# Attention in an fp32 encoder: the product of probabilities and v as plain fp32 on two 64-column halves of the array

## Chip, core and metric

The kernel runs on one core of one Trainium2 chip. The metric is device time in microseconds (us) of one execution, the median of several; lower is better. The output has to agree with a float32 reference.

The engines are named as the profile names them: PE is TensorE's matmul side, PEld its weight loads, DVE is VectorE, ACT ScalarE, POOL GpSimd, SP SyncE (which only issues DMAs here). In a matmul row, "128*128 128x256" means 128 rows by 128 columns of the array in use and a moving operand of 128 partitions by 256 elements.

## The reference

Two layers of an encoder over 512 tokens of width 1024, each a half-step FFN, a mixer of neighbourhood attention and a Fourier branch, and a second half-step FFN; a final RMSNorm. The change is in the attention: 8 heads of 64 channels on a grid of 8 rows by 64 columns of tokens. Queries come in 4 blocks of 16 grid columns, each with a band of 32 columns of keys. A block is 8 x 16 = 128 queries, a band 8 x 32 = 256 keys.

```python
s = jnp.einsum('brjqhd,brjuvhd->brjhquv', qg, k_win).astype(jnp.float32) * scale + bias[None]
s = jnp.where(col_ok[None, None, :, None, :, None, :], s, -jnp.inf)
sh = s.shape
p = jax.nn.softmax(s.reshape(sh[:-2] + (kh * KEY_BAND_COLS,)), axis=-1).reshape(sh)
o = jnp.einsum('brjhquv,brjuvhd->brjqhd', p.astype(v.dtype), v_win)
```

The last line is the product that the change touches: probabilities times the values of the band.

## The kernel before

**Numbers in two parts.** Nearly every product in the kernel is made in three passes. An operand x is split into a high part hi, which ScalarE writes in the type fp32r (a copy that rounds), and a low part lo = x - hi, which VectorE writes. `mm3` (L314 to L317) then issues hi*hi, hi*lo and lo*hi into one PSUM accumulation. `hilo` makes one buffer of 512 KB with room for both parts; all such buffers, and the weights of the mixer stage, share one pool of 23 buffers (tag "k", `slot`, L111). PSUM has 8 banks of 512 fp32 columns (`bank`, L118).

**Weights.** `ws` streams weights from HBM: SP and POOL issue the loads, ScalarE writes the high parts (whi), VectorE the low parts (wlo), a few granules ahead of TensorE.

**Attention in chunks.** The work comes in eight chunks i = 0 to 7: hp = i // 2 is a pair of heads (their 2 x 64 channels fill the 128 partitions) and pr = i % 2 a pair of query blocks. For each chunk the steps are:

- `att_scores` (L1264): scores of both heads. The two heads lie in the two halves of the partitions, so each matmul uses 64 rows of the array, and the calls alternate between the heads (e = 0, 1).
- `Probs`: bias, maximum, exponential, sum and scaling, on VectorE and ScalarE.
- `transposed` (L1311): eight fp32 transposes on TensorE (L1317) bring keys onto the partitions. For each of the two blocks jj, one PSUM bank then holds 512 columns: key half c = 0, 1, and in each half the 128 queries of head 0 and the 128 of head 1.
- `high_of` (L1094): ScalarE copies such a bank to SBUF as the high part (L1097), VectorE subtracts to make the low part (L1100). Both are named p.
- `att_pv` (L1324): for each block and key half, `mm3` with v as the stationary operand, 128 columns (both heads), and the 256 columns (both heads' queries) as the moving one: 12 matmuls of 256 columns a chunk. The result has a row of blocks of which only those with a head's own v and its own queries are used.
- `att_split` (L1336): picks these blocks out of PSUM, one ScalarE copy (L1342) and one VectorE subtraction (L1345) for each head, and writes the two parts of o.

**v.** A projection leaves four 128-token blocks of values. `v_high` (L1107) scales them into a high part on ScalarE (L1109), `v_low` (L1111) makes the low part on VectorE (L1112). Bands that straddle two blocks need a shifted copy: three buffers vs, each filled by two DMAs from SP (L1554, L1555).

**Order.** The whole attention stands in a manual schedule: the order of work on TensorE, VectorE and ScalarE is the order of the program text. Between the attention's steps stand the Fourier branch (`four_*`, `rotated`, `rows_of`), the projections (`proj_T`) and the preparation of weights. `att_pv` is called for two chunks in a row each time, so there are four such pairs in a layer: (0, 1) between the last key projection and transposes, the others among `rows_of`. Next comes the gate stage (`gate_block`), with products in the same three passes. `flip` (L475) holds a plain fp32 matmul, one call in each layer, with 2 moving columns.

Of the kernel before, what the change touches and what calls it, by code (L numbers as in the profile page):

```python
# [9 lines left out]
F32 = mybir.dt.float32  # L10
F32R = mybir.dt.float32r
# [23 lines left out]
BAND = (0, 1, 3, 4)  # L35
# [55 lines left out]
def encoder_kernel(  # L91
    ctx: ExitStack, tc: tile.TileContext, xin, xtr, wst, gains, gfin, gbias, bias_in, dft, chan, ident_in, rot, out
):
    nc = tc.nc
    V, S, G, PE = nc.vector, nc.scalar, nc.gpsimd, nc.tensor
# [218 lines left out]
    def mm3(ps, lh, ll, rh, rl, start, stop, again=False):  # L314
        PE.matmul(ps, lh, rh, start=start, stop=False, skip_group_check=again)  # L315
        PE.matmul(ps, lh, rl, start=False, stop=False, skip_group_check=again)  # L316
        PE.matmul(ps, ll, rh, start=False, stop=stop, skip_group_check=again)  # L317
# [717 lines left out]
    def stage_mixer(l, norm, nxt):  # L1035
# [58 lines left out]
        def high_of(t, s):  # L1094

            hi, lo = hilo(s)
            S.activation(hi, t, AF.Copy)  # L1097

            def low_of():
                V.tensor_tensor(lo, t, hi.bitcast(F32), ALU.subtract)  # L1100
                return hi, lo

            return low_of

        vt = [None] * TB

        def v_high(b, src):  # L1107
            vt[b] = slot(F32R, "v", (2, T))
            S.activation(vt[b][:, 0, :], src, AF.Copy, scale=norm.r[:, b : b + 1])  # L1109

        def v_low(b, src):  # L1111
            V.scalar_tensor_tensor(  # L1112
                vt[b][:, 1, :], src, norm.r[:, b : b + 1], vt[b][:, 0, :].bitcast(F32), ALU.mult, ALU.subtract
            )

        def proj_UV():

# [137 lines left out]
        o, q, k, bms = [], {}, {}, {}  # L1255
# [55 lines left out]
        def transposed(s_):  # L1311
# [9 lines left out]
                res.append(pt)  # L1321
            return res

        def att_pv(i, p_):  # L1324
            hp, pr = divmod(i, 2)
            po = bank()
            hs = slice(hp * P, (hp + 1) * P)
            for jj in range(2):
                ph, pl = p_[jj]
                for c in range(2):  # L1330
                    vh, vl = vch[BAND[2 * pr + jj] + 2 * c]
                    cs = slice(c * 256, (c + 1) * 256)
                    mm3(po[:, jj * 256 : jj * 256 + 256], vh[:, hs], vl[:, hs], ph[:, cs], pl[:, cs], c == 0, c == 1)
            return po

        def att_split(i, po):  # L1336
            hp, pr = divmod(i, 2)
            pv = po.rearrange("p (a e q) -> p a e q", a=2, e=2)
            oh, ol = [z[:, pr * 256 : pr * 256 + 256].rearrange("p (a q) -> p a q", a=2) for z in o[hp]]
            for e in range(2):  # L1340
                r = slice(64 * e, 64 * e + 64)
                S.activation(oh[r], pv[r, :, e, :], AF.Copy)  # L1342
            for e in range(2):
                r = slice(64 * e, 64 * e + 64)
                V.tensor_tensor(ol[r], pv[r, :, e, :], oh[r].bitcast(F32), ALU.subtract)  # L1345


        def rows_of(src, tb, w, kts=range(4), ps=None):
# [141 lines left out]
        with tc.manual_schedule(engines={mybir.EngineType.DVE, mybir.EngineType.Activation}):  # L1490
            with tc.manual_schedule(engines={mybir.EngineType.PE}):
                u, k1, pa, sb, acts4 = proj_UV()
# [24 lines left out]
                product(pa, acts4, K4, False, again=True, ahead=0)  # L1517
                q[2] = q2()
                for c in range(2):
                    v_high(c, pa[c])  # L1520
                f0, f1 = four_ch(b_[0]), four_ch(b_[1])
                g0, g1 = four_q(f0[1]), four_q(f1[1])
                for c in range(2):
                    v_low(c, pa[c])
                bias_for(1)
                p1.exps(1)
                fp = [four_pos(2), four_pos(3)]
# [3 lines left out]
                p1.inverse(1)  # L1531
                k2 = proj_T(None, 0)
                for c in range(2):
                    v_high(2 + c, sb[:, c, :])
                y0 = four_high(y0)
                y1 = four_high(y1)
                bt = [rotated(fp[0])]
# [8 lines left out]
                b_ = [bh[0](), bh[1]()]  # L1546
                k2 = k2()
                ws.prep(ws.pos + 2)
                for c in range(2):
                    v_low(2 + c, sb[:, c, :])  # L1550
                vs = []
                for s in range(3):
                    t = slot(F32R, "vs", (2, T))
                    nc.sync.dma_start(out=t[0:64].bitcast(F32), in_=vt[s][64:128].bitcast(F32))  # L1554
                    nc.sync.dma_start(out=t[64:128].bitcast(F32), in_=vt[s + 1][0:64].bitcast(F32))  # L1555
                    vs.append(t)
                fq = []

# [10 lines left out]
                w1 = four_high(w1)  # L1569
                yf += [y0(), y1()]  # L1570
                ts = transposed(p0.s) + transposed(p1.s)
                ph = [high_of(t, "p") for t in ts]
                q3 = q3()
                ph = [h() for h in ph]
                pt_ = {0: ph[0:2], 1: ph[2:4]}
                p2, p3 = [Probs(i, att_scores(i)) for i in (2, 3)]
                k3 = proj_T(None, 0)
                p2.maxes(0)
# [19 lines left out]
                p3.scaled(1)  # L1598
                k3 = k3(False)
                bias_for(2)  # L1600
                vch = {i: (t[:, 0, :], t[:, 1, :]) for i, t in ((0, vt[0]), (1, vs[0]), (2, vt[1]), (3, vs[1]), (4, vt[2]), (5, vs[2]), (6, vt[3]))}
# [6 lines left out]
                ph = [high_of(t, "p") for t in ts[0:2]]  # L1608
                pt_[2] = [h() for h in ph]
# [4 lines left out]
                pt_[3] = [h() for h in ph]  # L1614
# [28 lines left out]
                ph = [high_of(t, "p") for t in ts[0:2]]  # L1643
                pt_[4] = [h() for h in ph]
                att_split(2, po[0])
                att_split(3, po[1])
                second_f = [ws.next(0)]
# [1 line left out]
                p6.maxes(0)  # L1649
                ws.prep(ws.pos + 1)  # L1650
                p6.maxes(1)
                ph = [high_of(t, "p") for t in ts[2:4]]
                pt_[5] = [h() for h in ph]
                p6.exps(0)
                p7.maxes(0)
                p6.inverse(0)
# [24 lines left out]
                ph = [high_of(t, "p") for t in ts[0:2]]  # L1681
                pt_[6] = [h() for h in ph]
                att_split(4, po[0])
                att_split(5, po[1])
                ph = [high_of(t, "p") for t in ts[2:4]]
# [5 lines left out]
                po = [att_pv(i, pt_.pop(i)) for i in (6, 7)]  # L1691
# [61 lines left out]
        pa = pair("wA")  # L1753
# [230 lines left out]
```

## Time and profile before

| | |
|---|---|
| median of 3 timed runs | 1870.2 us (1869.01 to 1872.32) |
| profiled execution, device time | 1872.91 us |
| its span, first to last instruction | 1871.1 us |
| ScalarE busy in the span | 1307.7 us (70%) |
| granted TensorE clock, mean | 0.999 |
| HBM read over the span | 365.85 MB, 197 GB/s |

How to read it. The page of a profile gives busy time for each engine; a share of the span is a mean over stages that have different limits. Matmuls are pipelined: the next starts before the last has ended, so the cost of one is read from start to start, not from its own duration. Rows of the order of time read: start, duration, engine, line, operation, output and inputs by the program's names, shape, count; a row with "x24" stands for 24 like instructions in a row. In brackets stands the idle time ahead of a row and what ended it. The rows on which the argument rests stand in the prediction.

### The profile page before, as it was taken

To read this page: it belongs to the slowest core of one execution; us is meant where nothing else is said; L and a number is where in the kernel's file an instruction comes from. 1 tells how busy PE (TensorE), PEld (TensorE's weight loads), DVE (VectorE), ACT (ScalarE), POOL (GpSimd) and SP (SyncE) were. 2 spreads that over 40 slices of the span, in tenths; PEclk is the share of its full clock that TensorE was granted. 3 is DMA by queue.
4 is the path that set the end of the run, shared out by engine and by line. 5 is a ranking of instruction groups with operands and counts; after the bars stand their busy time and mean duration, and the time that the engine had idled before them with its cause. 6 is when DMAs were issued, how large, how long until landed. Compare 5 with 4: busy or idle time off the path is not lost.

```text
span 1871.1 us, 24628 instructions
## 1 busy us (share of the span) xinstructions
PE 1854.5 (99%) x8830; PEld 1543.7 (82%) x8830; DVE 1638.3 (88%) x2006; ACT 1307.7 (70%) x1788; POOL 171.4 (9%) x210
## 2 busy tenths in 40 slices
PE   9999999999999999999999999999999999999998
PEld 7888878888888888888888888878887888888886
DVE  7877899788989987889998888997889899888899
ACT  6777875668666867777666778666685567677865
POOL 0001011100111001001010100101001101010010
PEclk9999999999999999999999999999999999999999
DMA  9898798932886888879888887988248867888794
GB/s 302 223 236 210 196 255 271 230 103 90 248 219 161 179 225 225 223 195 259 259 196 220 225 219 200 269 266 202 85 139 229 213 166 176 221 227 222 196 283 151
DMA packets 190139, 393.70 MB, mean 210 GB/s; under 512 B 95488, under 2 KB 95616, under 8 KB 190016
## 3 DMA queue, kind: packets, MB, share of 16 engines
q1 hardware_dynamic: 161344, 293.77, 48.8%
q0 software_dynamic: 28528, 98.33, 29.6%
q8 instruction: 69, 1.13, 0.2%
q14 instruction: 54, 0.44, 0.1%
q10 hardware_dynamic: 144, 0.02, 0.0%
HBM read 365.85 MB, written 2.11 MB: 197 GB/s over the span
## 4 chain that ended last, share of the span: by engine, by line
PE 85%; DVE 5%; DMA 5%; issue 4%; ACT 1%; POOL 0%; SPq 0%; DVEq 0%; ACTq 0%; POOLq 0%
PE A L491 10%; PE A L492 10%; PE A L494 10%; PE B L492 5%; PE B L491 5%; PE B L494 5%; PE o L494 5%; PE o L492 5%; PE o L491 5%; DMA raw<-in_wst_dram 4%; PE ps L315 3%; PE ps L316 3%; PE ps L317 3%; PE C L491 2%; PE C L492 2%
## 5 line engine op out<-in xcount | busy, mean ns | idle before, releaser
L194 DVE TENSOR_TENSOR wlo<-raw,whi 128x1024 fp32r<-128x1024 f32 (+1 forms) x534 | 630.8, 1190 | 165.6 <-ACT whi L191 164.2
L191 ACT ACTIVATE whi<-raw 128x1024 fp32r<-128x1024 f32 (+1 forms) x534 | 547.2, 1033 | 270.5 <-DVE raw L164 59.8
L150 POOL DMA_DIRECT2D raw<-in_wst_dram x166 | 144.3, 889 | 1337.4 <-DMA raw<-in_wst_dram 895.5
L164 DVE TENSOR_TENSOR raw<-raw,raw 128x1024 f32<-128x1024 f32 (+1 forms) x150 | 178.5, 1191 | 2.0
L492 PE MATMUL A<-whi,xl 128*128 128x512 f32 x400 | 155.7, 389 | 0.0
L491 PE MATMUL A<-whi,xh 128*128 128x512 f32 x400 | 155.7, 389 | 0.0
L698 ACT ACTIVATE at<-zt 128x1024 uint16<-128x1024 uint16 (+2 forms) x96 | 111.0, 1168 | 20.6 <-DMA zt<-zs 20.6
L186 ACT ACTIVATE whi<-raw 128x1024 fp32r<-128x1024 f32 (+1 forms) x83 | 85.9, 1035 | 50.2 <-PE A L492 13.6
L494 PE MATMUL A<-wlo,xh 128*128 128x512 f32 x400 | 115.0, 389 | 0.0
L187 DVE SCALAR_TENSOR_TENSOR wlo<-raw,whi 128x1024 fp32r<-128x1024 f32 (+1 forms) x83 | 98.2, 1192 | 12.9 <-ACT whi L186 12.8
L494 PEld LDWEIGHTS A<-wlo,xh 128*128 128x128 f32 x400 | 75.1, 188 | 15.6
L491 PEld LDWEIGHTS A<-whi,xh 128*128 128x128 f32 x400 | 75.1, 188 | 15.4
L492 PEld LDWEIGHTS A<-whi,xl 128*128 128x128 f32 x400 | 75.1, 188 | 15.4
L491 PE MATMUL C<-whi,xh 128*128 128x512 f32 x208 | 81.3, 391 | 0.5 <-ACT whi L191 0.5
L492 PE MATMUL C<-whi,xl 128*128 128x512 f32 x208 | 81.0, 389 | 0.0
L492 PE MATMUL B<-whi,xl 128*128 128x512 f32 x208 | 81.0, 389 | 0.0
L491 PE MATMUL B<-whi,xh 128*128 128x512 f32 x208 | 80.9, 389 | 0.0
L681 ACT ACTIVATE zs<-th 128x1024 uint16<-128x1024 uint16 x80 | 79.5, 1042 | 0.9 <-DVE th L729 0.9
L722 ACT ACTIVATE th<-sn,rh 128x512 f32<-128x512 f32 x80 | 55.1, 715 | 35.4 <-DVE sn L566 34.6
L561 ACT ACTIVATE sn<-A 128x512 f32<-128x512 f32 x104 | 59.1, 585 | 23.6 <-PE A L494 23.6
L494 PE MATMUL C<-wlo,xh 128*128 128x512 f32 x208 | 59.8, 389 | 0.0
L494 PE MATMUL B<-wlo,xh 128*128 128x512 f32 x208 | 59.8, 389 | 0.0
(449 smaller groups left out, 4772.0 us busy)
## 6 DMA issues: line engine op xcount, KB each, us to landing
raw<-in_wst_dram SPq DMA_DIRECT2D x470, 512.0 KB, 5.7
raw<-in_wst_dram POOLq DMA_DIRECT2D x174, 512.0 KB, 8.0
raw<-in_wst_dram SPq DMA_DIRECT2D x30, 256.0 KB, 3.5
bm<-in_bias_dram SPq DMA_DIRECT2D x16, 384.0 KB, 3.8
vs<-v SPq DMA_DIRECT2D x12, 256.0 KB, 3.8
x<-in_xin_dram SPq DMA_DIRECT2D x4, 512.0 KB, 10.2
raw<-in_wst_dram POOLq DMA_DIRECT2D x8, 256.0 KB, 8.4
dft<-in_dft_dram POOLq DMA_DIRECT2D x8, 256.0 KB, 4.3
```

The costliest lines, as they stand in the source:

```text
L150: G.dma_start(out=self.t, in_=wst[GRAN_AT[self.plus]][:, 0 : self.n], accum_op=ALU.add)
L164: V.tensor_tensor(self.raw.t, self.raw.t, self.add.t, ALU.add)
L186: S.activation(hi, t, AF.Copy, scale=-1.0)
L187: self.last = V.scalar_tensor_tensor(lo, t, -1.0, hi.bitcast(F32), ALU.mult, ALU.subtract)
L191: S.activation(hi[:, cs], t[:, cs], AF.Copy)
L194: self.last = V.tensor_tensor(lo[:, cs], t[:, cs], hi[:, cs].bitcast(F32), ALU.subtract)
L491: PE.matmul(ps, lh, rh, start=start, stop=False, skip_group_check=again)
L492: PE.matmul(ps, ll, rh, start=False, stop=False, skip_group_check=again)
L494: PE.matmul(ps, lh, rl, start=False, stop=stop, skip_group_check=again)
L561: S.activation(t[:, b, :], ps[b], AF.Copy)
L681: S.activation(s[:, h], words[:, h], AF.Copy)
L698: S.activation(to[:, w, i : i + n, :], t[:, w, q : q + n, :], AF.Copy)
```

## The change

`att_pv` takes v and the probabilities as plain fp32. For each block and key half it issues one matmul for each head: 64 columns of v as the stationary operand, the head's own 128 queries as the moving one, and the output on partitions 0 to 63 or 64 to 127, the halves of the array's columns. A chunk has 8 such calls in place of 12 matmuls of three passes. The output of a chunk is 256 columns in which every block is used, so `att_split` is one copy and one subtraction over all partitions. v and p have no low parts any more: `value` and `kept` make plain fp32 copies on ScalarE. Buffers for v and vs hold half as many bytes, and p has one buffer for a chunk in place of two.

```diff
-        def v_high(b, src):
-            vt[b] = slot(F32R, "v", (2, T))
-            S.activation(vt[b][:, 0, :], src, AF.Copy, scale=norm.r[:, b : b + 1])
-
-        def v_low(b, src):
-            V.scalar_tensor_tensor(
-                vt[b][:, 1, :], src, norm.r[:, b : b + 1], vt[b][:, 0, :].bitcast(F32), ALU.mult, ALU.subtract
-            )
+        def value(b, src):
+            vt[b] = slot(F32, "v", (T,))
+            S.activation(vt[b], src, AF.Copy, scale=norm.r[:, b : b + 1])
...
+        def kept(ts):
+            p_ = slot(F32, "p", (2, T))
+            for jj in range(2):
+                S.activation(p_[:, jj, :], ts[jj], AF.Copy)
+            return p_
+
         def att_pv(i, p_):
             hp, pr = divmod(i, 2)
             po = bank()
-            hs = slice(hp * P, (hp + 1) * P)
             for jj in range(2):
-                ph, pl = p_[jj]
+                js = slice(jj * P, (jj + 1) * P)
                 for c in range(2):
-                    vh, vl = vch[BAND[2 * pr + jj] + 2 * c]
-                    cs = slice(c * 256, (c + 1) * 256)
-                    mm3(po[:, jj * 256 : jj * 256 + 256], vh[:, hs], vl[:, hs], ph[:, cs], pl[:, cs], c == 0, c == 1)
+                    v = vch[BAND[2 * pr + jj] + 2 * c]
+                    for e in range(2):
+                        d = slice(hp * P + 64 * e, hp * P + 64 * e + 64)
+                        cs = slice(c * 256 + e * P, c * 256 + (e + 1) * P)
+                        PE.matmul(po[64 * e : 64 * e + 64, js], v[:, d], p_[:, jj, cs], start=c == 0, stop=c == 1)
             return po
 
         def att_split(i, po):
             hp, pr = divmod(i, 2)
-            pv = po.rearrange("p (a e q) -> p a e q", a=2, e=2)
-            oh, ol = [z[:, pr * 256 : pr * 256 + 256].rearrange("p (a q) -> p a q", a=2) for z in o[hp]]
-            for e in range(2):
-                r = slice(64 * e, 64 * e + 64)
-                S.activation(oh[r], pv[r, :, e, :], AF.Copy)
-            for e in range(2):
-                r = slice(64 * e, 64 * e + 64)
-                V.tensor_tensor(ol[r], pv[r, :, e, :], oh[r].bitcast(F32), ALU.subtract)
+            oh, ol = [z[:, pr * 256 : pr * 256 + 256] for z in o[hp]]
+            S.activation(oh, po[:, 0:256], AF.Copy)
+            V.tensor_tensor(ol, po[:, 0:256], oh.bitcast(F32), ALU.subtract)
...
                 for c in range(2):
-                    v_high(2 + c, sb[:, c, :])
+                    value(2 + c, sb[:, c, :])
...
-                for c in range(2):
-                    v_low(2 + c, sb[:, c, :])
                 vs = []
                 for s in range(3):
-                    t = slot(F32R, "vs", (2, T))
-                    nc.sync.dma_start(out=t[0:64].bitcast(F32), in_=vt[s][64:128].bitcast(F32))
-                    nc.sync.dma_start(out=t[64:128].bitcast(F32), in_=vt[s + 1][0:64].bitcast(F32))
+                    t = slot(F32, "vs", (T,))
+                    nc.sync.dma_start(out=t[0:64], in_=vt[s][64:128])
+                    nc.sync.dma_start(out=t[64:128], in_=vt[s + 1][0:64])
                     vs.append(t)
...
                 ts = transposed(p0.s) + transposed(p1.s)
-                ph = [high_of(t, "p") for t in ts]
+                pt_ = {0: kept(ts[0:2]), 1: kept(ts[2:4])}
                 q3 = q3()
-                ph = [h() for h in ph]
-                pt_ = {0: ph[0:2], 1: ph[2:4]}
...
-                ph = [high_of(t, "p") for t in ts[2:4]]
-                pt_[7] = [h() for h in ph]
+                pt_[7] = kept(ts[2:4])
```

The calls for the other chunks change in the same way, at the places where they stood.

More of the change, by code (lines that the diff above doesn't have):

```diff
@@ L1519, in stage_mixer @@
                 for c in range(2):
-                    v_high(c, pa[c])
+                    value(c, pa[c])
                 f0, f1 = four_ch(b_[0]), four_ch(b_[1])
                 g0, g1 = four_q(f0[1]), four_q(f1[1])
-                for c in range(2):
-                    v_low(c, pa[c])
                 bias_for(1)
@@ L1548, in stage_mixer @@
                 ws.prep(ws.pos + 2)
-                for c in range(2):
-                    v_low(2 + c, sb[:, c, :])
                 vs = []
                 for s in range(3):
-                    t = slot(F32R, "vs", (2, T))
-                    nc.sync.dma_start(out=t[0:64].bitcast(F32), in_=vt[s][64:128].bitcast(F32))
-                    nc.sync.dma_start(out=t[64:128].bitcast(F32), in_=vt[s + 1][0:64].bitcast(F32))
+                    t = slot(F32, "vs", (T,))
+                    nc.sync.dma_start(out=t[0:64], in_=vt[s][64:128])
+                    nc.sync.dma_start(out=t[64:128], in_=vt[s + 1][0:64])
                     vs.append(t)
@@ L1600, in stage_mixer @@
                 bias_for(2)
-                vch = {i: (t[:, 0, :], t[:, 1, :]) for i, t in ((0, vt[0]), (1, vs[0]), (2, vt[1]), (3, vs[1]), (4, vt[2]), (5, vs[2]), (6, vt[3]))}
+                vch = dict(enumerate((vt[0], vs[0], vt[1], vs[1], vt[2], vs[2], vt[3])))
                 o.append(hilo("o"))
@@ L1607, in stage_mixer @@
                 ts += transposed(p3.s)
-                ph = [high_of(t, "p") for t in ts[0:2]]
-                pt_[2] = [h() for h in ph]
+                pt_[2] = kept(ts[0:2])
                 att_split(0, po[0])
@@ L1612, in stage_mixer @@
                 k3 = k3()
-                ph = [high_of(t, "p") for t in ts[2:4]]
-                pt_[3] = [h() for h in ph]
+                pt_[3] = kept(ts[2:4])
                 k[3] = k3()
@@ L1642, in stage_mixer @@
                 ts = transposed(p4.s) + transposed(p5.s)
-                ph = [high_of(t, "p") for t in ts[0:2]]
-                pt_[4] = [h() for h in ph]
+                pt_[4] = kept(ts[0:2])
                 att_split(2, po[0])
@@ L1651, in stage_mixer @@
                 p6.maxes(1)
-                ph = [high_of(t, "p") for t in ts[2:4]]
-                pt_[5] = [h() for h in ph]
+                pt_[5] = kept(ts[2:4])
                 p6.exps(0)
@@ L1680, in stage_mixer @@
                 swap_pools(0)
-                ph = [high_of(t, "p") for t in ts[0:2]]
-                pt_[6] = [h() for h in ph]
+                pt_[6] = kept(ts[0:2])
                 att_split(4, po[0])
                 att_split(5, po[1])
-                ph = [high_of(t, "p") for t in ts[2:4]]
-                pt_[7] = [h() for h in ph]
+                pt_[7] = kept(ts[2:4])
                 ws.prep(ws.pos + 1)
```

## The prediction

> **What bounds the kernel now.** I read the page first, then busy times by stretch, then the order of time on TensorE around the product.
>
> ```profile
> span 1871.1 us, 24628 instructions
> ...
> PE 1854.5 (99%) x8830; PEld 1543.7 (82%) x8830; DVE 1638.3 (88%) x2006; ACT 1307.7 (70%) x1788; POOL 171.4 (9%) x210
> ...
> PE 85%; DVE 5%; DMA 5%; issue 4%; ACT 1%; POOL 0%; SPq 0%; DVEq 0%; ACTq 0%; POOLq 0%
> ```
>
> TensorE is busy for 99% of the span and holds 85% of the chain of waits. An average hides stages, so the two stretches that hold the attention (one for each layer) come next, all instructions first, then those on the tiles named p alone.
>
> ```profile
> 380.00:500.00 120.00, 119.98 (x703) 102.94 (x702) 103.95 (x218) 85.91 (x188) 4.60 (x6) 1.00 0.43 131
> 1310.00:1430.00 120.00, 119.99 (x702) 102.91 (x701) 104.55 (x219) 85.45 (x187) 5.17 (x6) 1.00 0.45 134
> ```
>
> ```profile
> 380.00:500.00 120.00, 12.16 (x96) 12.06 (x96) 10.20 (x16) 8.54 (x16) 1.00 0.43 131
> 1310.00:1430.00 120.00, 12.15 (x96) 12.05 (x96) 10.21 (x16) 8.53 (x16) 1.00 0.45 134
> ```
>
> Columns: stretch, its length, busy time (count) of matmuls, weight loads, VectorE, ScalarE and in the first view GpSimd, then TensorE's granted clock (1.00: full), DMA share, GB/s. In both layers TensorE is covered to 0.02 us while VectorE and ScalarE have 16 and 34 us free. The product of p and v is 96 matmuls a layer. So what decides is how long TensorE takes over it; the rest counts only where TensorE waits for it.
>
> **What the product costs now.** Matmuls overlap their ends, so I count from start to start. This is the first pair of products (i = 0 and 1) with its neighbours in time.
>
> ```profile
> 429.36 0.39 PE L317 MATMUL ps<-xh,wlo 128*128 128x512 f32 x1
> 429.59 0.28 PE L315 MATMUL ps<-p,v 128*128 128x256 f32 x1
> ...
> 432.34 0.29 PE L317 MATMUL ps<-p,v 128*128 128x256 f32 x1
> 432.47 1.03 PE L1317 MATMUL ps<-ident,s 128*128 128x128 f32 x8
> 433.26 0.48 PE L315 MATMUL ps<-whi,y 128*128 128x512 f32 x1
> 433.57 0.39 PE L316 MATMUL ps<-wlo,y 128*128 128x512 f32 x1
> ```
>
> 24 matmuls of 256 columns run from 429.59 to 432.47: 2.88 us, 0.12 each. There are 4 such pairs a layer, 8 in all: 23.0 us. A matmul of 512 columns takes 0.23 (429.36 to 429.59).
>
> **What it costs after.** A pair becomes 2 x 8 calls of plain fp32 on 64 columns of the array and 128 moving columns. The kernel has one plain fp32 product already, in flip (one call a layer):
>
> ```profile
> L475 PEld LDWEIGHTS ps<-r,ident x4: 187/188/188, 376.0 to 1303.8; 128*128 128x128 f32 x4
> L475 PE MATMUL ps<-r,ident x4: 165/208/251, 376.2 to 1303.9; 128*128 128x2 f32 x4
> ```
>
> ```profile
> 376.20 0.19 PEld L475 LDWEIGHTS ps<-r,ident 128*128 128x128 f32 x1
> 376.30 0.19 PEld L315 LDWEIGHTS ps<-xh,whi 128*128 128x128 f32 x1
> 376.42 0.19 PEld L316 LDWEIGHTS ps<-xl,whi 128*128 128x128 f32 x1
> ```
>
> Two calls left 4 weight loads and 4 matmuls: one plain fp32 call is two load-matmul pairs. A pair of products is then 32 of them, 16 on each half of the array. With almost nothing to stream (2 columns), loads follow each other after 0.10 and 0.12 us: a load of 128 columns takes 0.11, and for 64 columns I take half, 0.055.
>
> How long one such matmul holds its half no row shows. The nearest in type and moving columns are the fp32 transposes L1317: from 432.47 to 433.57 are 1.10 us; less one 512-column matmul (0.23) that leaves 0.87 for 8, so 0.109 each. From below that cannot shrink by much, since a 64-column load (0.055) has to fit in; from above, the pace per moving element of a 256-column matmul gives 0.12, and twice the transposes' pace 0.22, about a 512-column matmul's 0.227 (a rival below). I take 0.109: same type, same 128 columns.
>
> [...]
>
> Do the halves work at once? The scores (L1276) already split the array, by rows, alternating between two halves:
>
> ```profile
> 396.34 0.39 PE L317 MATMUL ps<-xh,wlo 128*128 128x512 f32 x1
> 396.66 1.69 PE L1276 MATMUL ps<-q,q 64*128 64x256 f32 x24
> 398.29 0.50 PE L491 MATMUL A<-whi,t4h 128*128 128x512 f32 x1
> 398.62 0.40 PE L492 MATMUL A<-whi,t4l 128*128 128x512 f32 x1
> ```
>
> ```profile
> 396.66 0.38 PE L1276 MATMUL ps<-q,q 64*128 64x256 f32 x2
> ```
>
> 24 matmuls of 256 columns take 1.63 us, not 2.88, and a window of 0.02 us shows two starting together: row halves run in parallel. A split by columns no row shows; I let it do the same. But the new order is first half, first half, second half, second half, since both matmuls of a call go to one half. If matmuls start in order, the second of a call waits for the first, and the other half's first can start with it. So the halves run one slot apart, and 32 matmuls take 17 slots, not 16: 1.85 us.
>
> The split itself has a price. From 396.34 to 398.62 are 2.28 us; less 12 slots of 0.12 and two 512-column matmuls (0.45) that leaves 0.39 for going into the split and out. Between ends of 0 and 0.39 for a split by columns I take 0.39. The new pair: 1.85 + 0.39 = 2.24, which saves 0.64; times 8: **-5.1 us**.
>
> **Everything else.**
>
> ```profile
> L1100 DVE TENSOR_TENSOR p<-ps,p x32: 677/682/692, 423.2 to 1398.5; 128x512 fp32r<-128x512 f32 x32
> ...
> L1342 ACT ACTIVATE o<-ps x32: 367/378/382, 436.4 to 1401.4; 64x256 fp32r<-64x256 f32 x32
> ...
> L1345 DVE TENSOR_TENSOR o<-ps,o x32: 406/423/429, 437.3 to 1403.9; 64x256 fp32r<-64x256 f32 x32
> ...
> L1112 DVE SCALAR_TENSOR_TENSOR v<-A,r,v x4: 740/746/751, 404.9 to 1333.2; 128x512 fp32r<-128x512 f32 x4
> L1112 DVE SCALAR_TENSOR_TENSOR v<-sn,r,v x4: 744/745/746, 418.4 to 1346.7; 128x512 fp32r<-128x512 f32 x4
> ```
>
> VectorE loses 32 x 0.682 (low parts of p), 8 x 0.745 (of v) and 16 x 0.423 (o is split in 16 operations over all partitions): 34.6 us. ScalarE loses 16 x 0.378 = 6.0; the copies that made high parts stay as plain copies. I book nothing for it: the cover is TensorE at 119.98 of 120 us. If TensorE went off the path, that would be 17 us of VectorE a layer, a gain. The six shifted copies of v in a layer move half the bytes and no longer wait for v's low parts; the product comes 20 us later, so nothing changes. P takes one k buffer where it took two, so some weight loads can start earlier; TensorE does not wait for those. No wait is added: kept is one ScalarE copy where a copy and a VectorE subtraction stood.
>
> TensorE does wait behind this VectorE work once a layer:
>
> ```profile
> 437.06 2.07 PE L1276 MATMUL ps<-q,q 64*128 64x256 f32 x24
> 439.06 0.50 PE L315 MATMUL ps<-whi,y 128*128 128x512 f32 x1
> ```
>
> ```profile
>   DVE o L1345: 0.4, 2
> ```
>
> ```profile
> PE A L491 <- ACT sn L561: 1.9, 2, 1.1
> ```
>
> The scores of chunks 4 and 5 take 2.00 us in place of 1.63, waiting for a PSUM bank that the last subtraction of o frees (0.4 us, 2 times). With 4 subtractions made 2 and two low parts of p gone ahead of them, it should vanish: -0.37 a layer, **-0.7**. Two stalls stand in the gate stage (1.9 us in all). They sit behind a weight and a snapshot there, some 40 us after the attention; I leave them, and as a bound they could go too.
>
> **The sum**: -5.1 - 0.7 = -5.8 us. The span of 1871.1 becomes 1865.3, the profiled run (1872.91 us) 1867.1. That run stands 2.7 over the median of the three timed ones, 1870.2, so the prediction there is **1864.4 us**. Its own range: 0.12 a slot and no stall gained is 2.43 a pair, -3.6, 1866.6; a free split and both kinds of stall gone is -8.2 - 0.7 - 1.9 = -10.8, 1859.4.
>
> **The rivals.**
>
> *Half an overlap.* The halves run side by side, but the weights of the other half are not fetched ahead past a waiting matmul. Then each change of half shows its load: 0.109 + 0.055 + 0.109 + 0.055 = 0.328 for four matmuls, 2.62 a pair, 3.01 with the split: +0.13 x 8 - 0.7 = +0.3, 1870.5. For it: on the undivided array each load starts when the matmul ahead of it starts, never earlier (loads of L315 and L316 above, 376.30 and 376.42). Against it: row halves start two by two, which needs two loads fetched ahead. [...]
>
> *No overlap: slower.* Column halves take turns. For it: each half needs a moving stream of its own through the same 128 rows, which the row split never asks for. Against it: nothing in the trace but the likeness of the two splits. 32 x 0.109 + 0.39 = 3.88 a pair, +1.00 x 8 - 0.7 = +7.3, 1877.5; with 0.12, 4.23 and 1880.3. The break-even lies at about 23 slots of 0.109 a pair.
>
> *A dear slot: slower too.* The halves overlap but a plain matmul of 128 columns holds its half for 0.227. 17 x 0.227 + 0.39 = 4.25, +1.37 x 8 - 0.7 = +10.3, 1880.5. For it: L475 streams 2 columns and tells nothing of the pace, and a transpose is another operation. Without overlap as well, 7.65 a pair: 1907.7.
>
> **How the numbers follow.** The forecast gets 0.48, half an overlap 0.15, no overlap 0.23, the dear slot 0.14 (0.03 of it without overlap). A change is told from none by about 0.2%, 3.7 us: 1866.5 to 1873.9. The forecast is faster but for 0.01; half an overlap lies inside but for 0.01 on each side; the other two are slower. Faster 0.48, same 0.14, slower 0.38. The range of 1860 to 1881 takes in the first three with their bounds and the overlapped dear slot; some 0.07 stay outside.
>
> **What would show it.** In order of time, the first pair should take about 2.24 us from its first matmul to the transposes, with 32 matmuls of 64 columns, two for each call. About 2.9 to 3.0 means half an overlap; 3.9 no overlap; 4.2 a dear slot or a turn-taking one at 0.12, told apart by whether matmuls on the two halves start together. The step into and out of the split shows at its edges, and the scores of chunks 4 and 5 should be back at 1.63. VectorE's busy time should fall by about 35 us with little effect. The prediction is wrong if the pair takes over 2.5 us, or if TensorE gains waits outside the attention.

## The result, and the profile after

| | before | after |
|---|---|---|
| median, 4 runs each | 1870.36 us (1869.01 to 1872.32) | 1861.96 us (1859.98 to 1864.93) |
| ratio, 95% interval | | 0.9956, 0.9938 to 0.9973 |
| profiled execution | 1872.91 us, span 1871.1 | 1859.98 us, span 1858.2 |

The change makes the kernel 8.4 us faster; the interval of the ratio is 5.0 to 11.6 us. The two profiled executions lie 12.9 us apart, since the one of before is 2.5 over its median and the one of after 2.0 under. So a stretch is read below for what one place gained, and the medians for the whole.

The page of after, its first lines and the shares of the chain of waits:

```profile
span 1858.2 us, 24666 instructions
...
PE 1843.7 (99%) x8894; PEld 1533.9 (83%) x8894; DVE 1606.6 (86%) x1950; ACT 1300.2 (70%) x1772; POOL 171.3 (9%) x210
...
PE 97%; DVE 1%; ACT 1%; DMA 0%; issue 0%; SPq 0%; DVEq 0%
```

TensorE has 64 matmuls more (16 chunks by 16 in place of 12) and is still busy for 99% of a shorter span. VectorE lost 56 instructions, as forecast (32 + 8 + 16), and 31.7 us. TensorE's share of the chain of waits rose from 85% (89% in a second profile of before) to 97%: more than before, it alone sets the end.

The order of time on TensorE around the first two pairs of products (start, duration, engine, line, tile, shape, count):

```profile
428.15 0.39 PE L317 MATMUL ps<-xh,wlo 128*128 128x512 f32 x1
428.47 0.66 PE L1335 MATMUL ps<-p,v 128*64 128x128 f32 x8
428.96 1.04 PE L1335 MATMUL ps<-p,vs 128*64 128x128 f32 x16
429.83 0.61 PE L1335 MATMUL ps<-p,v 128*64 128x128 f32 x8
430.37 1.09 PE L1312 MATMUL ps<-ident,s 128*128 128x128 f32 x8
...
431.53 0.39 PE L316 MATMUL ps<-wlo,y 128*128 128x512 f32 x1
...
442.00 0.39 PE L317 MATMUL ps<-whi,y 128*128 128x512 f32 x1
442.31 0.66 PE L1335 MATMUL ps<-p,v 128*64 128x128 f32 x8
442.80 1.04 PE L1335 MATMUL ps<-p,vs 128*64 128x128 f32 x16
443.68 0.61 PE L1335 MATMUL ps<-p,v 128*64 128x128 f32 x8
444.21 0.50 PE L315 MATMUL ps<-whi,y 128*128 128x512 f32 x1
444.55 0.40 PE L316 MATMUL ps<-wlo,y 128*128 128x512 f32 x1
```

The second pair has 512-column matmuls on both sides and is the clean one: from 442.00 to 444.55 are 2.55 us; less two such matmuls (0.45), 2.10 for the pair with its way in and out. It was 2.88. A slot is the time from one start on a half to the next, 0.109 us in the prediction. From 442.31 to 443.68 start 24 matmuls in 1.37 us: 0.114 for two, close to one slot and far from two. 32 matmuls in 16 slots are 1.74, so the edges take 0.35. Eight pairs at 0.78 less are 6.2 us.

The whole attention of a layer, from the last matmul before the scores of chunk 0 to the first product with the high part of the o weights, in before (the start in layer 1 is the row of 396.34 in the prediction):

```profile
472.35 0.39 PE L315 MATMUL ps<-whi,o 128*128 128x512 f32 x1
...
1323.98 0.39 PE L317 MATMUL ps<-xh,wlo 128*128 128x512 f32 x1
...
1400.01 0.39 PE L315 MATMUL ps<-whi,o 128*128 128x512 f32 x1
```

and in after, with the scores of chunks 4 and 5:

```profile
395.14 0.39 PE L317 MATMUL ps<-xh,wlo 128*128 128x512 f32 x1
...
435.02 1.70 PE L1271 MATMUL ps<-q,q 64*128 64x256 f32 x24
436.65 0.50 PE L315 MATMUL ps<-whi,y 128*128 128x512 f32 x1
...
467.43 0.50 PE L315 MATMUL ps<-whi,o 128*128 128x512 f32 x1
...
1315.84 0.39 PE L317 MATMUL ps<-xh,wlo 128*128 128x512 f32 x1
...
1388.12 0.50 PE L315 MATMUL ps<-whi,o 128*128 128x512 f32 x1
```

Layer 1 went from 76.01 to 72.29 us, layer 2 from 76.03 to 72.28: 3.7 less in each, 7.5 in all. Four pairs give 3.1 of a layer's 3.7, and the scores of chunks 4 and 5, now 1.63 us where they took 2.00, another 0.4. The last 0.2 is made of three small parts: the scores of chunks 6 and 7 (1.68 became 1.63), the first pair, which saves 0.83 with the transposes behind it, and 0.1 at the last pair, whose way out lies behind the row at which the stretch ends.

Outside the attention, the waits of TensorE (in us, times, longest) have lost a row. The longest in after, which before has too:

```profile
PE o L492 <- DVE c1l L322: 1.6, 3, 0.5
```

The 1.9 us of the gate stage (A at L491 behind the snapshot sn) are gone. With them the places named come to 9.4 us in this pair of executions; the rest of the 12.9 lies outside them.

### The profile page after: what moved, and what is told of

It reads as the page before. It is cut to its first block, busy times and chain, and to the rows that moved or that the text cites. A ratio compares the mean times of both kernels' runs of the same rounds, so it can differ in the third digit from the quotient of the medians.

```text
span 1858.2 us, 24666 instructions
## 1 busy us (share of the span) xinstructions
PE 1843.7 (99%) x8894; PEld 1533.9 (83%) x8894; DVE 1606.6 (86%) x1950; ACT 1300.2 (70%) x1772; POOL 171.3 (9%) x210
## 4 chain that ended last, share of the span: by engine, by line
PE 97%; DVE 1%; ACT 1%; DMA 0%; issue 0%; SPq 0%; DVEq 0%
PE A L491 10%; PE A L492 10%; PE A L494 10%; PE o L492 7%; PE o L494 7%; PE o L491 7%; PE B L492 5%; PE B L491 5%; PE B L494 5%; PE ps L315 4%; PE ps L316 3%; PE ps L317 3%; PE C L492 3%; PE C L491 3%; PE C L494 3%; PE tr L396 1%
## 5 line engine op out<-in xcount | busy, mean ns | idle before, releaser
L491 PE MATMUL A<-whi,xh 128*128 128x512 f32 x400 | 155.8, 390 | 0.0
L491 PEld LDWEIGHTS A<-whi,xh 128*128 128x128 f32 x400 | 75.1, 188 | 15.4
L491 PE MATMUL C<-whi,xh 128*128 128x512 f32 x208 | 81.2, 390 | 0.0
L491 PE MATMUL B<-whi,xh 128*128 128x512 f32 x208 | 81.0, 390 | 0.0
```

## The experiments

The medians of before in the three sets of runs were 1869.62, 1870.35 and 1870.93 us; each ratio is to the before of its own set. "After" in a diff is the changed kernel.

### Does a half wait for the order of the program?

**e1_heads_in_turn**: all calls of one half of the array first, then those of the other.

```diff
-            for jj in range(2):
-                for c in range(2):
-                    for e in range(2):
+            for e in range(2):
+                for jj in range(2):
+                    for c in range(2):
```

> Edit: in att_pv the loop over heads goes outermost, so a chunk issues four calls on the first half of the array and then four on the second, in place of alternating. Work and buffers are the same. Theory (the halves overlap only when calls alternate, matmuls start in order): up to 32 slots of 0.109 us for a pair of chunks less about 3 at the changes of half, so 3.2 to 3.5 us plus the split's 0.35, against 2.10 in the changed kernel; +1.4 to +1.8 us on each of 8 pairs, the kernel at 1873 to 1877 us, slower than the changed one by 0.6 to 0.8%. Rival (what runs together are the two matmuls of one call, on one half): the pair stays at 2.10 us and the kernel at 1862.

Measured: 1866.29 us, ratio 0.9977 (0.9968 to 0.9987), between the two expectations. The order of time of its first pair:

```profile
428.46 0.65 PE L1335 MATMUL ps<-p,v 128*64 128x128 f32 x4
428.94 0.27 PE L1335 MATMUL ps<-p,vs 128*64 128x128 f32 x1
428.95 0.32 PE L1335 MATMUL ps<-p,v 128*64 128x128 f32 x1
429.05 0.27 PE L1335 MATMUL ps<-p,vs 128*64 128x128 f32 x1
...
430.96 1.09 PE L1312 MATMUL ps<-ident,s 128*128 128x128 f32 x8
```

Chunk 0 has four matmuls of p and v and then four of p and vs for the first half, and only then those of p and v for the second half. Yet one of the second half starts at 428.95, ahead of the first half's at 429.05. The product takes 428.46 to 430.96, 2.50 us, against 428.47 to 430.37, 1.90, in after: 0.60 more, which times 8 is 4.8, and the medians lie 4.3 apart. If starts kept the order of the program, two matmuls could share a slot only at the three changes of half, and a pair would need 29 slots, 3.2 us; were the halves free of any order, it would need 16. So the order of the program does not hold between the halves, but the second half gets only so far ahead: it starts when the first still has three of its eight matmuls to start. With calls that alternate, that is enough for 16 slots out of 32 matmuls.

### Is it plain fp32 or the split that gains?

**e2_wide_fp32**: plain fp32, but one call for both heads over the undivided array, with 256 moving columns; o is picked out of PSUM as before the change.

```diff
-                    for e in range(2):
-                        d = slice(hp * P + 64 * e, hp * P + 64 * e + 64)
-                        cs = slice(c * 256 + e * P, c * 256 + (e + 1) * P)
-                        PE.matmul(po[64 * e : 64 * e + 64, js], v[:, d], p_[:, jj, cs], start=c == 0, stop=c == 1)
+                    cs = slice(c * 256, (c + 1) * 256)
+                    PE.matmul(po[:, jj * 256 : jj * 256 + 256], v[:, hs], p_[:, jj, cs], start=c == 0, stop=c == 1)
```

> Edit: plain fp32 is kept, the halves are not: one call for both heads with 128 columns of v and 256 moving columns, as the shape was before, and att_split as before. Theory (the gain on TensorE comes from the halves, which leave out the unused blocks and overlap): 16 matmuls of twice the moving columns for a pair, 16 x 0.213 to 0.227 = 3.4 to 3.6 us and no cost of a split, against 2.88 before the change and 2.10 after it; the kernel at 1872 to 1876 us, about as slow as before or slower. Rival (plain fp32 is what gains, with fewer instructions than three passes): at most 2.2 us for a pair and 1862 to 1863.

Measured: 1875.51 us, ratio 1.0024 (1.0015 to 1.0033), as expected. Its first pair in the order of time:

```profile
428.39 1.02 PE L1333 MATMUL ps<-p,v 128*128 128x256 f32 x4
429.25 1.89 PE L1333 MATMUL ps<-p,vs 128*128 128x256 f32 x8
430.98 1.03 PE L1333 MATMUL ps<-p,v 128*128 128x256 f32 x4
431.84 0.93 PE L1312 MATMUL ps<-ident,s 128*128 128x128 f32 x7
```

16 matmuls of 256 columns take 428.39 to 431.84, 3.45 us: 0.216 each, twice the 0.109 of 128 columns. So eight plain calls over the undivided array cost more than the 24 matmuls of three passes (3.45 against 2.88). The gain is that of the split: each head's own queries alone are streamed, and the halves work at once. Three passes on the two halves were not run, so it is open whether they would have gained as well.

### What does a way in and out of the split cost?

**e6_two_trips**: the transposes of chunk 2 are put between the products of chunks 0 and 1, which makes one more way out and in for one pair of each layer.

```diff
-                po = [att_pv(i, pt_.pop(i)) for i in range(2)]
+                po = [att_pv(0, pt_.pop(0))]
                 ts = transposed(p2.s)
+                po.append(att_pv(1, pt_.pop(1)))
```

> Edit: the changed kernel, with the eight transposes of chunk 2 between att_pv of chunk 0 and of chunk 1 in place of after both, so that the first pair of a layer enters and leaves the halves twice. Theory (each trip into the split costs 0.35 us by the edges in the order of time): the stretch from the matmul ahead of the first product to the one behind the transposes takes 0.35 us more in each layer, +0.7 in all, 1862.7 us, which only the order of time can show. Rival (the edges are pipelining, nothing is lost): no difference in that stretch.

Measured: 1861.32 us, ratio 0.9946 (0.993 to 0.9963); two extra ways of a third of a us do not show in a median. They do in the order of time:

```profile
427.98 0.39 PE L317 MATMUL ps<-xh,wlo 128*128 128x512 f32 x1
428.30 0.66 PE L1335 MATMUL ps<-p,v 128*64 128x128 f32 x8
428.78 0.61 PE L1335 MATMUL ps<-p,vs 128*64 128x128 f32 x8
429.32 1.09 PE L1312 MATMUL ps<-ident,s 128*128 128x128 f32 x8
430.34 0.66 PE L1335 MATMUL ps<-p,vs 128*64 128x128 f32 x8
...
431.70 0.39 PE L316 MATMUL ps<-wlo,y 128*128 128x512 f32 x1
```

From L317 to L316 the same work takes 3.72 us where after takes 3.38 (428.15 to 431.53): 0.34 for one more way out and in, the 0.35 that the second pair of after has at its edges. The attention of the other layer is 0.34 longer too.

### Does the lighter load on VectorE matter?

The prediction booked nothing for the 34.6 us that VectorE loses. The next kernels cross the two parts of the change: one takes off the load alone, the others take the new product and put the load back.

**e7_relief_alone**: before, but the low parts of p and v are not made; the high parts stand in for them in the three passes. o is still split in halves, so the load falls by 23.1 us (1638.3 to 1615.2) where the change has 31.7.

```diff
         def high_of(t, s):
...
+                if s == "p":
+                    return hi, hi
...
-                for c in range(2):
-                    v_low(c, pa[c])
...
-                for c in range(2):
-                    v_low(2 + c, sb[:, c, :])
```

> Edit: the kernel before, with the low parts of p and of v left out; its three passes read the high parts in their place, so TensorE's work is that of before (2.88 us a pair) while VectorE loses 27.8 us. att_split stays as before. Putting VectorE's work back into the changed kernel cost 7.3 us (1869.2), so either of two things holds. Theory (VectorE and TensorE are near balance: relief pays little while TensorE is the longer, the saving on TensorE pays only with relief): at most the stalls that the kernel before shows, 0.7 in the scores and 1.9 to 2.2 in the gate stage, 1867 to 1869 us. Rival (VectorE's work was the cost all along, the halves add nothing): 1862 to 1863 us.

Measured: 1870.17 us, ratio 0.9997 (0.9987 to 1.0006): nothing that can be told from no change, and over the 1867 to 1869 that its theory gave. The scores of chunks 4 and 5 are short in it (1.62 us from their start to the next matmul), and the attention is 0.5 us shorter in each layer, but among its waits of TensorE stands

```profile
PE ps L316 <- DVE wlo L175: 1.0, 2, 0.5
```

This wait, for a low part of the o weights, is one that before does not list: its 1.0 us is about what the attention wins.

**e4_vector_work_back**: after, with as many VectorE and ScalarE operations as before; the differences go into a scratch tile that nobody reads, and o is split in halves of the partitions.

```diff
+        def gone(in0, in1):
+            V.tensor_tensor(sp.tile([P, T], BF16, tag="gone", name=nm("gone"), bufs=1), in0, in1, ALU.subtract)
...
-            S.activation(oh, po[:, 0:256], AF.Copy)
-            V.tensor_tensor(ol, po[:, 0:256], oh.bitcast(F32), ALU.subtract)
+            for e in range(2):
+                r = slice(64 * e, 64 * e + 64)
+                S.activation(oh[r], po[r, 0:256], AF.Copy)
+            for e in range(2):
+                r = slice(64 * e, 64 * e + 64)
+                V.tensor_tensor(ol[r], po[r, 0:256], oh[r].bitcast(F32), ALU.subtract)
```

> Edit: the changed kernel with the work that it took from VectorE and ScalarE put back in its old places: low parts of p and of v are computed into a scratch tile that nobody reads, and att_split is done in two halves. TensorE's work and the buffers stay as changed. Theory (the stalls that went, ahead of the gate stage's A matmuls and in the scores of chunks 4 and 5, went because VectorE was relieved): 0.9 and 1.3 us come back in the gate stages and some 0.3 us in the scores of each layer, the kernel at 1864 to 1866 us. Rival (they went because p holds half as many buffers, so that weights load earlier): the stalls stay away and the kernel is at 1862.

Measured: 1869.2 us, ratio 1.0002 (0.9992 to 1.0011). The gain is gone, though TensorE's products are those of after; no theory had expected that. Its scores of chunks 4 and 5, in the order of time with the idle time ahead of a row in brackets:

```profile
436.06 0.38 PE L1275 MATMUL ps<-q,q 64*128 64x256 f32 x1
436.66 1.18 PE L1275 MATMUL ps<-q,q 64*128 64x256 f32 x12 [0.22 <-DVE gone L1324]
438.22 0.97 PE L1275 MATMUL ps<-q,q 64*128 64x256 f32 x11 [0.38 <-DVE o L1361]
```

TensorE waits twice for a PSUM bank: until VectorE has read it for the low part, and until it has split o. The scratch writes were a little dearer than those of before (0.691 against 0.682 for p; the 0.745 in the next expectation is that of v, which took as long before the change).

**e8_low_parts** makes this load equal to that of before: real low parts of p and v, in the other half of their buffers, and o split in halves. The product is that of after and reads the first half of the buffers.

```diff
-            vt[b] = slot(F32, "v", (T,))
+            vt[b] = slot(F32, "v", (2, T))
...
+        def value_low(b, src):
+            lo = vt[b][:, 1, :].bitcast(F32R)
+            V.scalar_tensor_tensor(lo, src, norm.r[:, b : b + 1], vt[b][:, 0, :], ALU.mult, ALU.subtract)
...
-            p_ = slot(F32, "p", (2, T))
+            p_ = [slot(F32, "p", (2, T)) for _ in range(2)]
...
+                    V.tensor_tensor(p_[jj][:, 1, :].bitcast(F32R), ts[jj], p_[jj][:, 0, :], ALU.subtract)
```

> Edit: as e4_vector_work_back, with the low parts written in fp32r into the second half of the buffers where the kernel before had them, since there they took 0.745 us into the scratch tile in place of 0.682; att_split in two halves as there. Nobody reads the low parts. Theory (VectorE's amount of work is what takes the gain away): 1867 to 1869 us, with stalls of TensorE at the scores of chunks 4 and 5 and ahead of the gate stage's A matmuls. Rival (the scratch tile and its slower writes did it): 1862 to 1864 us.

Measured: 1867.07 us, ratio 0.9984 (0.9971 to 0.9997). Its scores:

```profile
435.54 1.51 PE L1275 MATMUL ps<-q,q 64*128 64x256 f32 x13
437.44 0.98 PE L1275 MATMUL ps<-q,q 64*128 64x256 f32 x11 [0.39 <-DVE o L1358]
438.34 0.50 PE L315 MATMUL ps<-whi,y 128*128 128x512 f32 x1
```

2.80 us, longer than the 2.00 of before with the same load on VectorE: TensorE comes to that point earlier, VectorE does not (the rows follow under the next heading). The four corners:

| median, us | VectorE's load of before | lighter load |
|---|---|---|
| three passes | 1870.4 | 1870.2 (e7) |
| plain fp32 on halves | 1867.1 (e8) | 1862.0 |

The new product alone is worth about 3 us (0.6 to 5.4 by its interval), the lighter load alone nothing that shows (in e7 without the part of it that lies in the split of o), both 8.4.

### Which part of the load?

Four kernels put parts of e8's load back on after, in buffers like e8's where there are low parts. **e10_split_in_halves** has only the split of o in halves (the copies and subtractions of e4's diff, of which the subtractions are shown):

```diff
...
+            for e in range(2):
+                r = slice(64 * e, 64 * e + 64)
+                V.tensor_tensor(ol[r], po[r, 0:256], oh[r].bitcast(F32), ALU.subtract)
```

> Edit: the changed kernel with att_split alone in two halves of 64 partitions (16 more copies on ScalarE, 16 more subtractions on VectorE over the kernel). Theory (the wait at the scores hangs on the end of att_split, which frees the bank, so the two more operations in the row show there): the scores of chunks 4 and 5 take 0.3 to 0.8 us more in each layer, 1862.5 to 1864 us. Rival (only the low parts of p matter): 1862 us.

**e11_p_low** has only the low parts of p:

```diff
...
+                    V.tensor_tensor(p_[jj][:, 1, :].bitcast(F32R), ts[jj], p_[jj][:, 0, :], ALU.subtract)
...
```

> Edit: the changed kernel with the low parts of p alone computed (32 subtractions, 21.8 us of VectorE), read by nobody; not those of v, and att_split in one piece. Theory: most of what e4_vector_work_back lost comes back here, 1865 to 1868 us. Rival (the split of o in halves is what hurts): 1862 to 1863 us.

**e12_lows_no_split** has those of p and of v:

```diff
...
+            V.scalar_tensor_tensor(lo, src, norm.r[:, b : b + 1], vt[b][:, 0, :], ALU.mult, ALU.subtract)
...
+                    V.tensor_tensor(p_[jj][:, 1, :].bitcast(F32R), ts[jj], p_[jj][:, 0, :], ALU.subtract)
...
```

> Edit: e8_low_parts (1867.1 us: all of VectorE's work put back) with att_split in one piece, as in the changed kernel: the low parts of p and of v are computed and read by nobody. Known: low parts of p alone 1862.1, att_split in halves alone 1863.7. Theory (the split in halves is the last link of the row that TensorE waits for, the low parts only push it back): without it 1862 to 1863.5 us. Rival (the low parts of v cost the rest): 1865 to 1866 us.

**e13_p_low_and_split** has those of p and the split in halves:

```diff
...
+                    V.tensor_tensor(p_[jj][:, 1, :].bitcast(F32R), ts[jj], p_[jj][:, 0, :], ALU.subtract)
...
+                V.tensor_tensor(ol[r], po[r, 0:256], oh[r].bitcast(F32), ALU.subtract)
```

> Edit: e8_low_parts without the low parts of v: the low parts of p are computed and att_split is done in halves. Theory (the two stand in one row ahead of the same bank and the same weights, so that they add up there and pay from a threshold on): 1865.5 to 1867 us, with the scores of chunks 4 and 5 at 1.9 us or more. Rival (each costs what it costs alone): 0.1 + 1.8 over 1862, so 1863.5 to 1864 us.

| | median, us | ratio (interval) | over after, us | scores of 4 and 5, us | attention over after, us a layer |
|---|---|---|---|---|---|
| after | 1861.96 | 0.9956 (0.9938 to 0.9973) | | 1.63 | |
| e11, p | 1862.1 | 0.9954 (0.9939 to 0.9969) | 0.1 | 1.71 | 0.1 |
| e10, split | 1863.74 | 0.9965 (0.9953 to 0.9976) | 1.8 | 1.63 | 0.0 |
| e12, p and v | 1863.81 | 0.9961 (0.9946 to 0.9976) | 1.9 | 2.37 | 0.9 |
| e13, p and split | 1864.91 | 0.9968 (0.9958 to 0.9978) | 3.0 | 2.16 | 0.7 |
| e8, all | 1867.07 | 0.9984 (0.9971 to 0.9997) | 5.1 | 2.80 | 1.3 |

The last column is the stretch from the last matmul before the scores of chunk 0 to the first product with o, as above; the two layers of a kernel agree in it within 0.04 us. The intervals of the ratios are 4 to 7 us wide, so single steps of the medians are not settled, and the 5 us of the whole load are rough; the last column is far steadier. The low parts of p, 18.4 us of VectorE's time (1625.0 against 1606.6), cost nothing alone, which the theory for e11 had not foreseen (its rival had the number). The split alone does not lengthen the scores, where it had been expected to; its wait turns up elsewhere, in the list of e10's waits, and from the first to the last product with o each layer takes 0.8 us longer than in after, 1.6 of its 1.8:

```profile
PE ps L316 <- DVE wlo L175: 1.1, 2, 0.6
```

The medians of e12 and e13 lie between their theories and their rivals. In e13 the scores wait, and so does the gate stage, though its profiled execution was the slowest of its ten (1869.6 us):

```profile
PE A L491 <- ACT sn L561: 3.7, 2, 2.0
```

Why the costs do not add up is seen in the rows of VectorE ahead of the scores of chunks 4 and 5. VectorE there makes the low parts of p for one chunk and then splits o of chunks 0 and 1, which frees PSUM banks that the scores need. Where this work starts, in before (whose scores start at 437.06, as the prediction shows):

```profile
436.05 1.29 DVE L1100 TENSOR_TENSOR p<-ps,p 128x512 fp32r<-128x512 f32 x2 [0.87 <-ACT p L1097]
```

in e8 (whose scores start at 435.54, above):

```profile
435.33 1.29 DVE L1330 TENSOR_TENSOR p<-ps,p 128x512 fp32r<-128x512 f32 x2 [0.87 <-ACT p L1326]
```

in e11, with the start of its scores:

```profile
434.74 1.29 DVE L1326 TENSOR_TENSOR p<-ps,p 128x512 fp32r<-128x512 f32 x2 [0.87 <-ACT p L1322]
...
435.61 1.78 PE L1271 MATMUL ps<-q,q 64*128 64x256 f32 x24
```

and in e12:

```profile
436.73 1.29 DVE L1330 TENSOR_TENSOR p<-ps,p 128x512 fp32r<-128x512 f32 x2 [0.88 <-ACT p L1326]
...
436.94 0.38 PE L1275 MATMUL ps<-q,q 64*128 64x256 f32 x1
```

The table has how far ahead of the scores VectorE starts, how long the scores take, and the sum of the two:

| | VectorE ahead of the scores, us | scores, us | sum |
|---|---|---|---|
| before | 1.01 | 2.00 | 3.01 |
| e13, p and split | 0.85 | 2.16 | 3.01 |
| e8, all | 0.21 | 2.80 | 3.01 |
| e11, p | 0.87 | 1.71 | 2.58 |
| e12, p and v | 0.21 | 2.37 | 2.58 |

The sum is 3.01 wherever o is split in halves and 2.58 where it is not, and the same in the other layer within 0.02; the 0.43 between them is about one more subtraction (0.42). (e4, with its scratch writes, has 3.20.) So in these five kernels the scores end a fixed time after VectorE starts this work, however early TensorE comes. From before to e8 TensorE comes 0.80 earlier against VectorE, and the scores take 0.80 longer: what the first pair saves, 0.83, is lost again there. The low parts of v, 1.41 us of VectorE's time some 18 us earlier, hold VectorE back by 0.64 (e13 to e8) and 0.66 (e11 to e12). Without low parts of p, in after and e10, VectorE begins to split o at least 1.2 us ahead of the scores, and they take 1.63. Of e8's 5.1 us the attention accounts for 2 x 1.3 = 2.7; the rest, in waits that differ between executions, is not placed.

### Buffers, and the spread of before

**e5_two_buffers**: after, with p in two buffers for a chunk, as before the change.

```diff
-            p_ = slot(F32, "p", (2, T))
+            p_ = [slot(F32, "p", (T,)) for _ in range(2)]
```

> Edit: the changed kernel with p in two buffers of the k pool for a chunk, as before the change, each half used; nothing else. Theory (relief of VectorE took the stalls): no change, 1862 us, gate stalls absent. Rival (the freed buffers did): the gate stage's stalls of 0.9 and 1.3 us come back, 1864 us.

Measured: 1861.53 us, ratio 0.9954 (0.9938 to 0.9971). The freed buffers give nothing that shows.

**again_before**: the kernel before once more, for a second profile.

> The kernel before, unchanged, profiled once more: which of its waits come again. Theory (the waits that the change took belong to the kernel): the scores of chunks 4 and 5 take 2.00 us again and the gate stages lose 0.9 to 1.3 us each ahead of the A matmuls, whatever the weights' loads did in that execution. Rival (the gate stage's waits were this one execution's): they are absent or far smaller.

Measured: 1870.39 us, span 1868.6, 2.5 shorter than the first profile. The scores of chunks 4 and 5 and the gate stage in it:

```profile
436.39 2.09 PE L1276 MATMUL ps<-q,q 64*128 64x256 f32 x24
438.41 0.50 PE L315 MATMUL ps<-whi,y 128*128 128x512 f32 x1
```

```profile
PE A L491 <- ACT sn L561: 1.2, 1, 1.2
```

The wait at the scores is there in both executions (2.02 and 2.00 us), the one in the gate stage once in place of twice. The first belongs to the kernel, the second in part to the execution.

## Why the prediction was right, and where its sizes were off

**Direction and mechanism.** Forecast were 1864.4 us, and a range of its own of 1859.4 to 1866.6; measured are 1861.96. The halves do overlap, and nothing of what TensorE saves is lost outside the attention.

**The slot.** 0.109 us for 128 moving columns was taken from the transposes and holds: in the first pair of after the 16 matmuls of p and vs take 8 slots from 428.96 to 429.83, 0.109 each, 16 slots are 1.74 us, and e2 has 0.216 for 256. The dear slot (0.227) falls. The 0.12 in the range and in the rivals is the time of a 256-column matmul of the three passes; no run shows it for a plain fp32 matmul of 128 columns, which took 0.109.

**17 slots.** This step failed, though by little: "If matmuls start in order, the second of a call waits for the first" gave halves that run one slot apart. In after the two halves start together from the first slot on (428.468 and 428.474 for the first pair), and e1 shows that the halves are not held to the program's order (428.95 ahead of 429.05). 16 slots in place of 17 are 0.11 a pair. Half an overlap and no overlap fall by the same rows: 32 matmuls with their loads take 16 slots, 2.10 us a pair where those two needed 3.01 and 3.88.

**The split's price.** Taken as 0.39 from the row split of the scores, measured as 0.35 in after and 0.34 in e6. With the slots the pair is 2.10 where 2.24 was forecast, and the term is -6.2 us where it was -5.1.

**The scores of chunks 4 and 5.** -0.37 a layer, as forecast: 2.00 became 1.63, in the place and for the reason that was given (e4 and e8 bring the wait back, with VectorE's splitting of o ahead of its end).

**The gate stage.** Left as it was, with 1.9 us as a bound. In the profiled executions the bound came true; again_before, with 1.2, says that part of it is the execution's. With -1.2 to -1.9 for it the sum is -8.1 to -8.8, and the medians give -8.4.

**VectorE booked at nothing.** "The cover is TensorE at 119.98 of 120 us" was true of before, and e7 agrees: the lighter load alone gains nothing that the medians show. But the cover was made thinner by the same change. With the saving on TensorE in place, the old load on VectorE would have taken back some 5 of 8.4 us (e8), 2.7 of 7.5 inside the attention alone. The forecast came out well because the change takes both away; its argument named TensorE's saving as nearly the whole cause, and alone that keeps about 3 us. In this the forecast was lucky: a version of the change that had to keep the low parts would have been forecast wrongly.

**Smaller readings.** VectorE lost 31.7 us, not 34.6: rows that follow one another overlap (two low parts of p take 1.29, not 2 x 0.682), so the low parts of p are 18.4 us and not 21.8. The last shifted copies of v were issued at 420.45 and used at 430.30, some 10 us later and not 20; nothing hung on it.

## What to carry to other kernels

When work is taken off the engine that sets the end, look at each place where it waits, or nearly waits, for another engine. The other engine does not come earlier there, so what the first saves ahead of that place can come back as a wait (0.80 us here, from before to e8), and a load that was free before is not free after. The busy share of a window does not show it; the starts of the two engines' rows at that place do. A product whose output is half unused may be cheaper in plain fp32 on two column halves than in three passes over the whole array (2.10 against 2.88 us a pair here), if the calls alternate between the halves (0.60 us a pair was lost where they did not) and stay together, since each way in and out cost 0.35 us.

## What the runs showed of the hardware

- Two column halves work at once though both use all 128 rows: 32 fp32 matmuls of 128 moving columns in 16 slots of 0.109 us (after: 16 of them in 8 slots from 428.96 to 429.83).
- They are not held to one order. In e1 the second half starts (428.95) while the first half still has three matmuls to start that come earlier in the program (the next at 429.05); the rest of the overlap is lost, 0.6 us a pair.
- A way out of the split into the undivided array and back costs 0.35 us in after, 0.34 in e6.
- A plain fp32 call is two load-matmul pairs, at 0.109 us for 128 moving columns (after) and 0.216 for 256 (e2), each. Three passes took 0.12 each for 256 (before). On the undivided array the plain call was the dearer of the two (3.45 in e2 against 2.88 us in before for the same product).
